# The transfers of a chunked recurrence through DRAM, moved from ACT's queue to GpSimd's with another scratch layout, in a two-layer trunk on one core

## The chip, the cores and the metric

The kernel runs on one core of a Trainium2 chip. What counts is the device time of one execution in microseconds. The engines are PE (matrix products), DVE (vector work), ACT (scalar work and casts), GpSimd, which the profile calls POOL, and SP, which here issues DMAs only. A DMA is issued by an instruction in the queue of one engine and carried out by 16 DMA engines that all queues share.

## What is computed

The input x has 256 rows of 2048 values in f32. Layer 0 adds a mixer of two kinds of heads, layer 1 a dilated attention, and each layer ends with an MLP of inner width 8192:

```python
for l in range(DEPTH):                    # DEPTH = 2
    if l % 2 == 0:
        x = x + diff_delta_mixer(rms_norm(x, ab_norm[i]), ...)
    else:
        x = x + dilated_mixer(rms_norm(x, c_norm[i]), ...)
    x = x + squared_relu_mlp(rms_norm(x, mlp_norm[l]), mlp_w1[l], mlp_w2[l])
```

The part that the change touches is the gated delta rule of the 8 "b" heads of layer 0, in chunks (cut):

```python
m = jnp.einsum('bhncd,bhnjd->bhncj', kb, k) * decay_strict
sol = lax.linalg.triangular_solve(eye + m, rhs, left_side=True, lower=True, unit_diagonal=True)
u, w = sol[..., :dv], sol[..., dv:]
def step(state, xs): ...                  # the state goes from chunk to chunk
```

## The kernel before

All dense products run through `dense` (L191): the weights are loaded by `wload` (L171) on SP's queue, cast on ACT to a high part (L204, tiles ending in h) and on DVE to a low part (L205, shown as L107 since the helper `tt` stands there, tiles ending in l), and each chunk of 128 rows takes six matmuls of 128x512 on PE (L210 to L212). High and low parts have six buffers each. After each chunk `drip` (L182) runs one step of the side work, which is held as generators in three streams. A scheduler then puts the instructions of each engine in an order of its own; each engine works through its own order strictly.

The recurrence is the generator `gdn` (L594), called four times (s = 0 to 3, tiles g0.. to g3..), each for two heads and two blocks of 128 rows, so four matrices of 128x128. A call goes as follows. `dd` holds the decays: a row of cumulative gates, written to DRAM once as scg (L530), is read back to all partitions (L623). `pk` is the product of the keys with themselves, and DVE makes `m` from it (L648). `m` is written to the scratch scm in DRAM (L651) and its 16x16 blocks on the diagonal, 8 to a matrix and 32 in all, are read into `mb`, one block to a partition (four DMAs, L654). DVE inverts the 32 blocks (`xc`, L673 to L695; a copy at L695 makes the transposed half). The inverses and their transposes are written into the block diagonals of the scratch scx, which was filled with zeros in `gates` (L534 to L536), by eight DMAs (L698), and the whole of scx is read back as `xy` (L704). From there three levels of PE products (`lp`, `ly`, `lx`, L720 on) build the whole inverse; the first is `lp16`, named g0lp and so on in the profile. Before the change all these DMAs are issued by ACT, whose queue also holds the casts of the weights. scm and scx are tiles of 128 partitions in which the four matrices (and in scx both halves) stand side by side in a row, so that a block diagonal is one pattern only per matrix.

The names beside it: z0, av0, av1, a1, wo00 are dense products of the mixer, c0 to c3 the convolutions (side work, with small memsets on GpSimd), d0 to d3 the other kind of heads (large memsets d0kb to d3kb on GpSimd), xq the input tiles, ca the constants, grow a row of gains, b0 the first dense product.

Of the kernel before, what the change touches and what calls it, by code (L numbers as in the profile page):

```python
# [11 lines left out]
F32 = mybir.dt.float32  # L12
# [7 lines left out]
P = 128  # L20
# [7 lines left out]
BLK = 16  # L28
# [59 lines left out]
def trunk(  # L88
# [4 lines left out]
    nc = tc.nc  # L93
    V, S, G, E = nc.vector, nc.scalar, nc.gpsimd, nc.tensor
# [5 lines left out]
    dp = ctx.enter_context(tc.tile_pool(name="dp", bufs=1, space=bass.MemoryType.DRAM))  # L100
# [5 lines left out]
    def tt(o, a, b, op):  # L106
        V.tensor_tensor(out=o, in0=a, in1=b, op=op)  # L107

    def vcopy(o, a):
        V.tensor_copy(out=o, in_=a)  # L110

    def stt(o, a, s, b, op0, op1):
        V.scalar_tensor_tensor(out=o, in0=a, scalar=s, in1=b, op0=op0, op1=op1)

    def ts(o, a, s1, s2, op0, op1=None):
        if op1 is None:
            V.tensor_scalar(out=o, in0=a, scalar1=s1, scalar2=None, op0=op0)
        else:
            V.tensor_scalar(out=o, in0=a, scalar1=s1, scalar2=s2, op0=op0, op1=op1)

    def act(o, a, f, scale=1.0, bias=0.0, accum=None):
        if accum is None:
            S.activation(out=o, in_=a, func=f, scale=scale, bias=bias)  # L123
        else:
            S.activation(out=o, in_=a, func=f, scale=scale, bias=bias, accum_out=accum)
# [4 lines left out]
    def ps_t(name):  # L130
        return pst.tile([P, 512], F32, tag="t", name=name)

    def ps_m(name):
        return psm.tile([P, 512], F32, tag="m", name=name)
# [36 lines left out]
    def wload(wsrc, k0, nm):  # L171
        raw = wp.tile([P, 2, 512], F32, tag="wr", name=f"{nm}r{k0}")
        off = 0
        for s in wsrc:
            m = s.shape[1]
            nc.sync.dma_start(raw[:, :, off:off + m], s[k0 * P:(k0 + 2) * P, :].rearrange("(c p) n -> p c n", p=P))
            off += m
        return raw
# [47 lines left out]
    ca = cp.tile([P, NMAIN], F32, name="ca")  # L226

    def cst(name):
        lo, hi = COLS[name]
        return ca[:, lo:hi]  # L230
# [3 lines left out]
    def transpose(o, i, k=P):  # L234
        E.transpose(o, i, ident[:k, :k])
# [12 lines left out]
    def x_tile(n, nm):  # L248
        return cp.tile([P, NH, 512], F32, tag=f"x{n}", name=f"{nm}{n}")
# [93 lines left out]
    xv = x[0].rearrange("(h p) d -> p h d", p=P)  # L343
# [3 lines left out]
    def b_cols(s):  # L347
        return [win[:, 3072 + s * 256:3328 + s * 256], win[:, 4096 + s * 256:4352 + s * 256]]

    grow0 = sp.tile([16, P], F32, tag="junk", name="grow0")  # L350
# [8 lines left out]
    xq = [x_tile(n, "xq") for n in range(4)]  # L359
    pre = []  # L360
    for n in range(4):
        if n == 0:
            nc.sync.dma_start(xq[0][:, :, :256], xv[:, :, :256])
            nc.sync.dma_start(ca[:, :P], consts[:, :P])
            nc.sync.dma_start(grow0, ab_norm[0].rearrange("(c p) -> c p", p=P))
            nc.sync.dma_start(xq[0][:, :, 256:], xv[:, :, 256:512])
        else:
            nc.sync.dma_start(xq[n], xv[:, :, n * 512:(n + 1) * 512])
        if n < 3:
            pre.append(wload(b_cols(0), 2 * n, "b0"))  # L370
    with ExitStack() as mix:
        wq[0] = mix.enter_context(tc.tile_pool(name="wq0", bufs=1))
        op = mix.enter_context(tc.tile_pool(name="op", bufs=1))
# [87 lines left out]
        gout = gt[:, 65:66]  # L461
        ready = set()
        oa, ob = [None] * 4, [None] * 4
        scm = [dp.tile([P, 512], F32, name=f"scm{i}") for i in range(2)]
        scg = dp.tile([16, P], F32, name="scg")
        scx = [dp.tile([P, 1024], F32, name=f"scx{i}") for i in range(2)]


        sz = [None] * NH
# [16 lines left out]
        def flat(a):  # L486
            return a.rearrange("p h n -> p (h n)")

        def gates(a, b):
            ts(beta, b, 0.5, 0.5, ALU.mult, ALU.add)  # L490
            ts(nbeta, beta, -1.0, None, ALU.mult)
            tt(a, a, dtb.unsqueeze(1).broadcast_to([P, NH, 8]), ALU.add)

            ab = mp.tile([P, NH, 8], F32, name="gab")
            y = mp.tile([P, NH, 8], F32, name="gy")
            w = mp.tile([P, NH, 8], F32, name="gw")
            q = mp.tile([P, NH, 8], F32, name="gq")
            stt(ab, a, -1.0, a, ALU.mult, ALU.min)
            act(y, ab, AF.Exp)
            ts(w, y, 2.0, None, ALU.add)  # L500
            V.reciprocal(out=w, in_=w)
            tt(w, y, w, ALU.mult)
            tt(y, w, w, ALU.mult)
            ts(q, y, 1.0 / 17.0, 1.0 / 15.0, ALU.mult, ALU.add)
            for d in (13, 11, 9, 7, 5, 3, 1):
                tt(q, q, y, ALU.mult)
                ts(q, q, 1.0 / d, None, ALU.add)
            yield
            tt(q, q, w, ALU.mult)
            ts(a, a, 0.0, None, ALU.max)  # L510
            stt(a, q, 2.0, a, ALU.mult, ALU.add)
            tt(gg, a, nega.unsqueeze(1).broadcast_to([P, NH, 8]), ALU.mult)
            yield
            yield
            pc = ps_m("pgc")
            E.matmul(pc[:, 0:16], lhsT=cst("tri"), rhs=flat(gg), start=True, stop=True)
            E.matmul(pc[:, 16:32], lhsT=cst("ones"), rhs=flat(gg), start=True, stop=True)
            vcopy(flat(gc), pc[:, 0:16])
            act(flat(egc), pc[:, 0:16], AF.Exp)
            e = sp.tile([P, 16], F32, tag="rs_z", name="ge")  # L520
            tt(e, pc[:, 16:32], flat(gc), ALU.subtract)
            act(flat(egl), e, AF.Exp)
            ngc = sp.tile([P, 16], F32, tag="ngc", name="ngc")
            ts(ngc, flat(gc), -1.0, None, ALU.mult)
            yield
            pc = ps_t("pgt")
            transpose(pc[:16, :P], ngc)
            row = sp.tile([P, 512], F32, tag="junk", name="grow_t")[:16, :P]
            vcopy(row, pc[:16, :P])
            nc.scalar.dma_start(scg, row)  # L530
            ready.add("gates")
            yield
            zero = mp.tile([P, 1024], F32, tag="xy", name="zero")
            G.memset(zero, 0.0)  # L534
            for z in scx:
                nc.sync.dma_start(z, zero)  # L536
            yield
            ready.add("zero")

# [54 lines left out]
        def gdn(qks, s, vb, nm):  # L594

            def mt(tag, n=4, share=None):
                return mp.tile([P, n, P], F32, tag="g_" + (share or tag), name=nm + tag)
# [19 lines left out]
            for i in range(4):  # L617
# [2 lines left out]
            ts(sq, rs[:, 4:8], 128.0 ** -0.5, None, ALU.mult)  # L620

            dd = mt("dd")
            nc.scalar.dma_start(  # L623
                dd.rearrange("p (h e) c -> p h e c", h=NH),
                bass.AP(scg.tensor, scg.offset + 2 * s * P, [[0, P], [8 * P, NH], [P, 2], [1, P]]))
            for i, (h, e) in enumerate(tiles):
# [6 lines left out]
            t = ps_t(nm + "kt")  # L633
# [8 lines left out]
            m, am = mt("m"), mt("am")  # L642
# [5 lines left out]
                stt(m[:, i, :], pk[:, i * P:(i + 1) * P], nbeta[:, h, hd:hd + 1], dd[:, i, :], ALU.mult, ALU.mult)  # L648

            scr, sxy = scm[s % 2], scx[s % 2]  # L650
            nc.scalar.dma_start(scr, m.rearrange("p i c -> p (i c)"))  # L651
            mb = mp.tile([32, BLK, BLK], F32, tag="g_mb", name=nm + "mb")
            for i in range(4):
                nc.scalar.dma_start(  # L654
                    mb[i * 8:(i + 1) * 8],
                    bass.AP(scr.tensor, scr.offset + i * P, [[BLK * 512 + BLK, 8], [512, BLK], [1, BLK]]))
            yield
            mT, aT = mt("mT"), mt("aT")
            t = ps_t(nm + "tt1")
# [5 lines left out]
            xc = mp.tile([32, 2, BLK, BLK], F32, tag="g_P", name=nm + "xc")  # L665
# [9 lines left out]
            for j in range(3):  # L675
                n, w = 3 - j, j + 1
# [16 lines left out]
                if b == 4:  # L693
                    yield
            vcopy(xc[:, 1].rearrange("p r c -> p c r"), x0)  # L695
            for i in range(4):
                for q in range(2):
                    nc.scalar.dma_start(  # L698
                        bass.AP(sxy.tensor, sxy.offset + q * 512 + i * P,
                                [[BLK * 1024 + BLK, 8], [1024, BLK], [1, BLK]]),  # L700
                        xc[i * 8:(i + 1) * 8, q])

            xy = mp.tile([P, 2, 4, P], F32, tag="xy", name=nm + "xy")
            nc.scalar.dma_start(xy.rearrange("p q i c -> p (q i c)"), sxy)  # L704
            X, Y = xy[:, 0], xy[:, 1]
            yield
            pa = ps_m(nm + "pa")
# [5 lines left out]
            t = ps_t(nm + "tt2")  # L713
# [5 lines left out]
            for li, b in enumerate(LEVELS):  # L719
                t = ps_m(f"{nm}lp{b}")  # L720
# [5 lines left out]
                t = ps_m(f"{nm}ly{b}")  # L726
# [4 lines left out]
                t = ps_t(f"{nm}lx{b}")  # L731
# [4 lines left out]
            t = ps_m(nm + "lpz")  # L736
# [5 lines left out]
            t = ps_m(nm + "lyz")  # L742
# [7 lines left out]
            t = ps_m(nm + "pu")  # L750
# [3 lines left out]
            t = ps_m(nm + "pw")  # L754
# [5 lines left out]
            t = ps_m(nm + "ps")  # L760
# [7 lines left out]
            t = ps_m(nm + "pv")  # L768
# [9 lines left out]
            t = ps_m(nm + "po")  # L778
# [406 lines left out]
```

## Time and profile before

| | |
|---|---|
| median of three runs | 2303.09 us (2300.97 to 2303.63) |
| the profiled execution | 2305.11 us, its span 2303.4 us |
| busy: PE / DVE / ACT / GpSimd | 2285.2 / 1666.8 / 1192.3 / 5.6 us |
| mean granted TensorE clock | 0.998 |
| DMA traffic | 426.54 MB, of it 4.60 MB on ACT's queue |

The span is the time between the first and the last record of the profiled execution; that execution took 1.7 us more than its span. Busy times are sums over the whole program. A view of stretches gives the busy time of each engine in a window, so that a window's length less PE's busy time is PE's idle time there; PEclk is the TensorE clock granted in it, as a share of full speed. The timeline gives single instructions, and for an instruction that issues a DMA the time of the issue, not of the transfer. The four recurrences lie between 75 and 450 us, the rest is other dense work and the two MLPs.

### The profile page before, as it was taken

Reading aid. Unit: us, or ns where it says so; the run is one execution under the profiler, and the core shown is the slowest. Engines: PE = TensorE matmul, PEld = TensorE weight load, DVE = VectorE, ACT = ScalarE, POOL = GpSimd, SP = SyncE. Lnnn points to the kernel's source line nnn. Section 1 sums busy time; section 2 is a strip of 40 time slices with the busy share of each in tenths; the row PEclk is TensorE's granted clock in tenths of the full one; section 3 lists DMA queues with packets and bytes.
Section 4 is the critical chain, followed back from the end, with each engine's and each line's share of the span. In section 5 each row is a group of like instructions: output and inputs, shape, how many; then the busy total and the mean of one; then the engine's idle time right before and its main releaser. Section 6 shows DMA issues by size and latency. Waiting matters only on the chain.

```text
span 2303.4 us, 29959 instructions
## 1 busy us (share of the span) xinstructions
PE 2285.2 (99%) x10544; PEld 1891.9 (82%) x10544; DVE 1666.8 (72%) x3027; ACT 1192.3 (52%) x1865; POOL 5.6 (0%) x15
## 2 busy tenths in 40 slices
PE   9999999999999999999999999999999999999999
PEld 8887878788888888888888888888888888888887
DVE  6767787777856856856888888986775775775774
ACT  7656756655534534534545555555543543443553
POOL 0000000000000000000000000000000000000000
PEclk9999999999999999999999999999999999999999
DMA  8655554466666666666666555555666666666665
GB/s 257 186 173 152 148 166 143 129 192 176 192 199 191 190 196 194 189 200 192 189 195 200 174 182 170 176 185 166 193 193 195 192 194 193 190 197 195 188 208 164
DMA packets 264762, 426.54 MB, mean 185 GB/s; under 512 B 22514, under 2 KB 94372, under 8 KB 264612
## 3 DMA queue, kind: packets, MB, share of 16 engines
q1 hardware_dynamic: 255812, 420.04, 60.0%
q10 hardware_dynamic: 8800, 4.60, 0.7%
q8 instruction: 82, 1.34, 0.3%
q14 instruction: 68, 0.56, 0.1%
HBM read 420.11 MB, written 4.46 MB: 184 GB/s over the span
## 4 chain that ended last, share of the span: by engine, by line
PE 92%; DVE 4%; DMA 2%; ACT 1%; issue 0%; ACTq 0%; SPq 0%; DVEq 0%
PE m_0p L211 3%; PE m_0p L212 3%; PE n_0p L212 3%; PE m_1p L210 3%; PE m_3p L210 3%; PE m_2p L210 3%; PE n_1p L212 3%; PE m_3p L212 3%; PE n_2p L211 3%; PE m_1p L212 3%; PE n_1p L211 3%; PE m_2p L212 3%; PE n_0p L210 3%; PE n_2p L210 3%; PE n_2p L212 3%; PE n_1p L210 3%
## 5 line engine op out<-in xcount | busy, mean ns | idle before, releaser
L107 DVE TENSOR_TENSOR n_2l<-n_2r,n_2h 128x1024 fp32r<-128x1024 f32 x64 | 78.4, 1226 | 76.8 <-ACT n_2h L204 76.7
L107 DVE TENSOR_TENSOR n_3l<-n_3r,n_3h 128x1024 fp32r<-128x1024 f32 x64 | 78.4, 1225 | 76.7 <-ACT n_3h L204 76.6
L107 DVE TENSOR_TENSOR m_0l<-m_0r,m_0h 128x1024 fp32r<-128x1024 f32 x64 | 78.1, 1225 | 73.4 <-ACT m_0h L204 73.0
L107 DVE TENSOR_TENSOR n_1l<-n_1r,n_1h 128x1024 fp32r<-128x1024 f32 x64 | 78.4, 1224 | 67.7 <-ACT n_1h L204 67.2
L204 ACT CAST n_2h<-n_2r 128x1024 fp32r<-128x1024 f32 x64 | 67.4, 1053 | 100.3 <-PE n_2p L212 61.6
L204 ACT CAST n_3h<-n_3r 128x1024 fp32r<-128x1024 f32 x64 | 67.3, 1052 | 100.2 <-PE n_3p L212 60.0
L204 ACT CAST m_0h<-m_0r 128x1024 fp32r<-128x1024 f32 x64 | 67.0, 1053 | 97.3 <-PE m_0p L212 59.9
L204 ACT CAST n_1h<-n_1r 128x1024 fp32r<-128x1024 f32 x64 | 67.4, 1053 | 92.8 <-PE n_1p L212 60.0
L107 DVE TENSOR_TENSOR m_1l<-m_1r,m_1h 128x1024 fp32r<-128x1024 f32 x64 | 78.4, 1225 | 36.9 <-ACT m_1h L204 35.9
L204 ACT CAST m_1h<-m_1r 128x1024 fp32r<-128x1024 f32 x64 | 67.4, 1053 | 66.6 <-PE m_1p L212 38.3
L204 ACT CAST m_3h<-m_3r 128x1024 fp32r<-128x1024 f32 x64 | 67.4, 1053 | 57.4 <-PE m_3p L212 39.9
L204 ACT CAST n_0h<-n_0r 128x1024 fp32r<-128x1024 f32 x64 | 67.4, 1053 | 57.3 <-PE n_0p L212 39.9
L204 ACT CAST m_2h<-m_2r 128x1024 fp32r<-128x1024 f32 x64 | 67.4, 1053 | 57.3 <-PE m_2p L212 39.9
L107 DVE TENSOR_TENSOR m_3l<-m_3r,m_3h 128x1024 fp32r<-128x1024 f32 x64 | 78.4, 1225 | 25.7 <-ACT m_3h L204 24.3
L107 DVE TENSOR_TENSOR n_0l<-n_0r,n_0h 128x1024 fp32r<-128x1024 f32 x64 | 78.4, 1225 | 25.7 <-ACT n_0h L204 24.0
L107 DVE TENSOR_TENSOR m_2l<-m_2r,m_2h 128x1024 fp32r<-128x1024 f32 x64 | 78.4, 1225 | 25.7 <-ACT m_2h L204 23.8
L293 DVE STREAM_TRANSPOSE m_0hT<-m_0r 32x256 f32<-32x256 f32 x128 | 55.8, 436 | 5.8 <-ACT m_0r L123 3.7
L293 DVE STREAM_TRANSPOSE m_2hT<-m_2r 32x256 f32<-32x256 f32 x128 | 55.8, 436 | 5.7 <-ACT m_2r L123 3.6
L293 DVE STREAM_TRANSPOSE m_3hT<-m_3r 32x256 f32<-32x256 f32 x128 | 55.8, 436 | 5.7 <-ACT m_3r L123 3.6
L293 DVE STREAM_TRANSPOSE m_1hT<-m_1r 32x256 f32<-32x256 f32 x128 | 55.8, 436 | 5.7 <-ACT m_1r L123 3.6
L210 PE MATMUL n_0p<-n_0h,m_3hh 128*128 128x512 f32 x64 | 24.9, 389 | 0.0
L210 PE MATMUL n_3p<-n_3h,m_1hh 128*128 128x512 f32 x64 | 24.9, 389 | 0.0
(2555 smaller groups left out, 7401.0 us busy)
## 6 DMA issues: line engine op xcount, KB each, us to landing
m_0r<-in_mlp_w_dram SPq DMA_DIRECT2D x64, 512.0 KB
m_1r<-in_mlp_w_dram SPq DMA_DIRECT2D x64, 512.0 KB
m_2r<-in_mlp_w_dram SPq DMA_DIRECT2D x64, 512.0 KB
m_3r<-in_mlp_w_dram SPq DMA_DIRECT2D x64, 512.0 KB
n_0r<-in_mlp_w_dram SPq DMA_DIRECT2D x64, 512.0 KB
n_1r<-in_mlp_w_dram SPq DMA_DIRECT2D x64, 512.0 KB
n_2r<-in_mlp_w_dram SPq DMA_DIRECT2D x64, 512.0 KB
n_3r<-in_mlp_w_dram SPq DMA_DIRECT2D x64, 512.0 KB
```

What stands on the lines that cost most here:

```text
L107: V.tensor_tensor(out=o, in0=a, in1=b, op=op)
L204: cast[0] = S.copy(whs, w)
L210: E.matmul(o, lhsT=sh, rhs=wh, start=kc == first, stop=False)
L211: E.matmul(o, lhsT=sh, rhs=wl, start=False, stop=False)
L212: E.matmul(o, lhsT=sl, rhs=wh, start=False, stop=kc == last)
L293: V.transpose(out=dv[:, :, :, q], in_=sv[:, :, :, j, :])
```

## The change

At the head, the loads of ca and grow go to ACT's queue, and the second half of the first input tile is issued after the first weights. In the mixer the scratch tiles become rows of images: scm has four and scx eight images of 128x128 with a pad of 128 behind each, so that the step from one block to the next on the diagonal also leads from the last block of one image to the first of the next. With that, all 32 blocks are one pattern (`DIAG`), the four reads of mb one DMA and the eight writes of scx two. The writes and reads of whole images now have runs of 512 B. All DMAs of the recurrence (scg, dd, scm, mb, scx, xy) are issued by GpSimd (`G`). For each call of `gdn` these are 15 DMAs before and 6 after.

```diff
-            nc.sync.dma_start(ca[:, :P], consts[:, :P])
-            nc.sync.dma_start(grow0, ab_norm[0].rearrange("(c p) -> c p", p=P))
-            nc.sync.dma_start(xq[0][:, :, 256:], xv[:, :, 256:512])
+            nc.scalar.dma_start(ca[:, :P], consts[:, :P])
+            nc.scalar.dma_start(grow0, ab_norm[0].rearrange("(c p) -> c p", p=P))
...
+        if n == 0:
+            nc.sync.dma_start(xq[0][:, :, 256:], xv[:, :, 256:512])
...
-        scm = [dp.tile([P, 512], F32, name=f"scm{i}") for i in range(2)]
+        IMG, DIAG = P * P + P, [[BLK * (P + 1), 32], [P, BLK], [1, BLK]]
+        scm = [dp.tile([4, IMG], F32, name=f"scm{i}") for i in range(2)]
-        scx = [dp.tile([P, 1024], F32, name=f"scx{i}") for i in range(2)]
+        scx = [dp.tile([8, IMG], F32, name=f"scx{i}") for i in range(2)]
+        def images(t):
+            return t[:, :P * P].rearrange("i (p c) -> p i c", c=P)
...
-            nc.scalar.dma_start(scg, row)
+            G.dma_start(scg, row)
...
-                nc.sync.dma_start(z, zero)
+                nc.sync.dma_start(images(z), zero.rearrange("p (i c) -> p i c", c=P))
...
-            nc.scalar.dma_start(
+            G.dma_start(
                 dd.rearrange("p (h e) c -> p h e c", h=NH),
...
-            nc.scalar.dma_start(scr, m.rearrange("p i c -> p (i c)"))
+            G.dma_start(images(scr), m)
-            for i in range(4):
-                nc.scalar.dma_start(
-                    mb[i * 8:(i + 1) * 8],
-                    bass.AP(scr.tensor, scr.offset + i * P, [[BLK * 512 + BLK, 8], [512, BLK], [1, BLK]]))
+            G.dma_start(mb, bass.AP(scr.tensor, scr.offset, DIAG))
...
-            for i in range(4):
-                for q in range(2):
-                    nc.scalar.dma_start(
-                        bass.AP(sxy.tensor, sxy.offset + q * 512 + i * P,
-                                [[BLK * 1024 + BLK, 8], [1024, BLK], [1, BLK]]),
-                        xc[i * 8:(i + 1) * 8, q])
+            for q in range(2):
+                G.dma_start(bass.AP(sxy.tensor, sxy.offset + q * 4 * IMG, DIAG), xc[:, q])
-            nc.scalar.dma_start(xy.rearrange("p q i c -> p (q i c)"), sxy)
+            G.dma_start(xy.rearrange("p q i c -> p (q i) c"), images(sxy))
```

The order of the instructions changes with it. On PE, around the first matmul of `lp16` in the third call (g2lp; av1p is the output of the dense product av1, av1h and av1l its weights), before:

```order
L210 MATMUL av1p_3628<-av1h_3840,xa3h 128x512
L211 MATMUL av1p_3628<-av1l_3841,xa3h 128x512
L212 MATMUL av1p_3628<-av1h_3840,xa3l 128x512
L210 MATMUL av1p_3627<-av1h_3857,xa3h 128x512 [waits Activation_49]
L722 MATMUL g2lp_3739<-g2xy,g2mT 128x128 [waits DMAHW6_49]
L722 MATMUL g2lp_3739<-g2xy,g2mT 128x128 x3
L211 MATMUL av1p_3627<-av1l_3858,xa3h 128x512 [waits DVE_49]
```

and after, on the same engine at the same matmul:

```order
L210 MATMUL av1p_3601<-av1h_3719,xa1h 128x512
L211 MATMUL av1p_3601<-av1l_3720,xa1h 128x512
L212 MATMUL av1p_3601<-av1h_3719,xa1l 128x512
L721 MATMUL g2lp_3712<-g2xy,g2mT 128x128 [waits DMASW3_49]
L721 MATMUL g2lp_3712<-g2xy,g2mT 128x128 x3
L210 MATMUL av1p_3600<-av1h_3735,xa2h 128x512 [waits Activation_49]
L211 MATMUL av1p_3600<-av1l_3736,xa2h 128x512 [waits DVE_49]
```

Before, the product stood among the last quarter of av1 (input block xa3); after, it stands between its second and third quarter (xa1 and xa2). From `pk` of the same call to this place there are 145 dense matmuls before and 114 after; in g0 118 and 108, in g1 108 and 108, in g3 95 and 73.

On ACT, around the scatters of the third call, before (8x16x16 is one of the eight writes of scx, CAST are high parts of av1):

```order
L204 CAST av1h_3778<-av1r_3760 128x512 [waits DVE_49,PE_49]
L698 DMA scx_228<-g2xc 8x16x16 [waits DMAHW4_49,DVE_49]
L698 DMA scx_228<-g2xc 8x16x16 [waits DMAHW5_49,DVE_49]
L698 DMA scx_228<-g2xc 8x16x16 x2
L698 DMA scx_228<-g2xc 8x16x16 [waits DMAHW2_49]
L698 DMA scx_228<-g2xc 8x16x16 [waits DMAHW3_49]
L698 DMA scx_228<-g2xc 8x16x16 [waits DMAHW4_49]
L698 DMA scx_228<-g2xc 8x16x16 [waits DMAHW5_49]
L204 CAST av1h_3793<-av1r_3791 128x512 [waits DMAHW1_49,PE_49]
```

and on GpSimd after, the rows of the third call:

```order
L657 DMA scm_225<-g2m 128x4x128 [waits DVE_49]
L877 MEMSET d1kb 128x1024 [waits DVE_49,Pool_49]
L659 DMA g2mb<-scm_225 32x16x16 [waits DMASW6_49,DMASW1_49]
L629 DMA g3dd<-scg 128x2x256 [waits DMASW2_49,DVE_49]
L700 DMA scx_228<-g2xc 32x16x16 [waits DVE_49] x2
L703 DMA g2xy<-scx_228 128x8x128 [waits DMASW2_49,DMASW5_49,DMASW1_49,PE_49]
```

The scatters stand no longer between two casts; on GpSimd they stand behind a memset and the load of the next call's decays. In the first call `g1dd` stands between the scatters and g0xy in the same way, in the second `g2dd` ahead of the scatters. ACT's order holds no DMA behind the head any more.

## Rows read from the trace of the kernel before

**Rows 1.** The page: busy us of the engines, share of the span, instructions.

```profile
PE 2285.2 (99%) x10544; PEld 1891.9 (82%) x10544; DVE 1666.8 (72%) x3027; ACT 1192.3 (52%) x1865; POOL 5.6 (0%) x15
```

**Rows 2.** Stretches of 25 us: length, PE, PEld, DVE, ACT, POOL busy, PEclk, DMA share, GB/s.

```profile
0.00:25.00 25.00, 22.56 (x114) 18.56 (x115) 15.98 (x32) 17.59 (x40) 1.20 (x6) 1.00 0.89 290
300.00:325.00 25.00, 21.89 (x99) 17.01 (x97) 20.54 (x62) 11.77 (x21) 0.00 (x0) 1.00 0.62 181
325.00:350.00 25.00, 24.46 (x125) 19.82 (x126) 17.57 (x44) 15.95 (x43) 0.95 (x1) 0.93 0.52 165
400.00:425.00 25.00, 21.27 (x86) 15.78 (x85) 17.75 (x56) 11.70 (x29) 0.95 (x1) 0.86 0.30 95
```

**Rows 3.** The same view from `pk` to `lp16` in g0, g1, g2, g3.

```profile
100.34:133.16 32.82, 31.69 (x160) 25.90 (x158) 28.39 (x64) 18.43 (x34) 0.76 (x2) 1.00 0.58 172
189.78:225.98 36.20, 34.47 (x174) 27.39 (x173) 29.03 (x89) 20.11 (x50) 0.11 (x1) 1.00 0.57 164
288.90:330.90 42.00, 38.35 (x170) 30.51 (x169) 37.13 (x95) 18.55 (x31) 0.95 (x1) 0.96 0.64 189
386.70:424.80 38.10, 34.31 (x153) 26.00 (x152) 28.12 (x91) 18.48 (x46) 0.95 (x1) 0.91 0.39 123
```

**Rows 4.** Timeline of ACT in g2, its DMA issues: start us, us, what.

```profile
296.00 0.35 ACTq L651 DMA_DIRECT2D scm<-g2m  x1
299.09 1.45 ACTq L654 DMA_DIRECT2D g2mb<-scm  x4
317.29 3.96 ACTq L698 DMA_DIRECT2D scx<-g2xc  x8
323.71 0.35 ACTq L704 DMA_DIRECT2D g2xy<-scx  x1
```

**Rows 5.** Instructions of tile g2xc: durations in ns, first and last start in us.

```profile
L113 DVE SCALAR_TENSOR_TENSOR g2xc<-g2mb,ca x1: 415/415/415, 306.2 to 306.2; 32x256 f32<-32x256 f32 x1
L110 DVE COPY g2xc<-g2xc x1: 368/368/368, 317.8 to 317.8; 32x256 f32<-32x256 f32 x1
```

**Rows 6.** The chain of three stretches (head, g0, g2): start us, us, what.

```profile
3.68 6.25 DMA xq<-in_x_dram
108.41 0.23 PE z0p L210
128.54 4.57 DMA g0xy<-scx
312.19 1.05 DVE g2tm L107
313.23 0.60 DVE av1l L107
```

**Rows 7.** Waits of ACT, then of PE: us in total, times, longest.

```profile
ACT av1h L204 <- DVE d1uw L107: 8.2, 1, 8.2
PE av1p L211 <- DVE av1l L107: 3.2, 2, 2.8
```

**Rows 8.** ACT's DMA queue, 121.7:128.6, 136.2:141, 128.5:133.3 us: packets, MB, share.

```profile
q10 hardware_dynamic: 1088, 0.07, 10.6%
q10 hardware_dynamic: 272, 0.26, 18.1%
q10 hardware_dynamic: 144, 0.52, 28.4%
```

**Rows 9.** GpSimd's instructions by shape: busy us, mean ns, idle before.

```profile
L878 POOL MEMSET d1kb<- 128x1024 f32 x1 | 1.0, 955 | 38.6 <-DVE qk L113 38.6
L534 POOL MEMSET zero<- 128x1024 f32 x1 | 1.0, 951 | 0.0
L553 POOL MEMSET c0x<- 128x16 f32 x1 | 0.1, 111 | 0.3 <-POOLq L1171 0.3
```

**Rows 10.** Timeline of the SP queue in the head: start us, us, what.

```profile
1.22 0.46 SPq L364 DMA_DIRECT2D ca<-in_consts_dram  x1
3.68 0.47 SPq L368 DMA_DIRECT2D xq<-in_x_dram  x1
```

## What the change will do to the time: the prediction

> **What bounds the kernel now.** I read the page first, then the busy time of 25-us stretches, then the stretches around the four recurrences, and only then the waits in them. TensorE (PE) is busy 2285.2 of 2303.4 us [rows 1]: what makes PE wait counts, nothing else does. The stretches say where PE is not busy: 2.4 us in the first 25 us, then 3.1, 0.5 and 3.7 us and a lowered clock around the third and fourth recurrence [rows 2]; these stretches hold over half of PE's 18.2 us of idle time. The change touches just these two places, the head and the four calls of `gdn` (g0 to g3), and the rest of the span I take as a constant.
>
> In each call I take the stretch from the start of `pk`, the first matmul of the recurrence, to the first matmul of `lp16`, which needs what comes back from DRAM: 32.8, 36.2, 42.0 and 38.1 us, with PE busy 31.7, 34.5, 38.4 and 34.3 of them [rows 3]. The reader is to see that two things run side by side there. One is PE's other work, the dense matmuls put ahead of `lp16`. The other is a chain: `pk`, `m`, write of scm, reads of mb, the triangular inverse on DVE (xc), writes of scx, read of xy. The later of the two sets the time.
>
> **The chain, in g2.** scm is issued at 296.00, 7.1 us after the start of the stretch; the first mb read at 299.09 (A, 3.1 us); xc begins on DVE at 306.17 (B, 7.1); its last copy starts at 317.8 and takes 0.37 (C, 12.0 from the start); xy is issued at 323.71 (D, 5.5) [rows 3 to 5]. A read of xy took 4.57 in g0 (E) [rows 6]; I use 4.6. What the transfers cost is S = A+B+D+E = 20.3 us. The same sum for g0, g1 and g3 (three calls, same lines) is 17.9, 19.3 and 18.7. The time from the start of the stretch to the scm issue is 3.2, 5.6, 7.1 and 5.2. In g2 xy had landed by 328.3 and `lp16` came at 330.9: there the chain was hidden behind dense work.
>
> **What the change does to S, link by link.** A: 512 packets of 512 B in place of 128 of 2 KB. The scatters' packets of 64 B took 10.7 ns each (10.6% of 16 engines for 6.9 us over 1088) and the 272 packets of dd, nearly all of 1 KB, 51 ns (18.1% of 16 engines for 4.8 us) [rows 8]; xy's 144 took 21.8 us in all, 151 ns each. Between the first two, 512 packets on 16 engines are 0.3 to 1.6 us; 128 at half of xy's price are 0.6 now. I take +0.5. B: four issues become one; they took 1.45 for four [rows 4], so -1.1. The runs stay 64 B. D: eight issues become two, 3.96 us in all with a wait at the first [rows 4]; six fewer at about 0.33 are -1.9. E: 1024 packets of 512 B in place of 128 of 4 KB; by the same rows 0.7 to 3.3 us against 1.4 now, so -0.7 to +1.9; I take +0.8. So far -1.7.
>
> Then the engine that issues. No row shows a DMA issued by GpSimd; its own instructions take 0.11 us for a small memset and 0.955 for a large one [rows 9], an issue on ACT 0.35 [rows 4]. Four issues lie one behind the other in the chain (scm, mb, the second scatter, xy). At 0.11 they give back 1.0 us, at 0.955 they cost 2.4. I take the upper end, since each DMA has 512 or 1024 pieces, which is nearer to the memset that writes much. S then goes up by 0.7 a call. The bounds: S-4.0 (A and E unchanged, GpSimd at 0.11), and S+4.9 from the rival on DVE below.
>
> Descriptor cost as the Trainium skill has it ("DMA: Bandwidth & Descriptors", Latency and other measured facts): about 1 us to the first byte from GpSimd, about 0.6 from ACT. By it four links would cost 1.6 rather than 2.4 and the total would come out about 3 us lower; no run here shows it.
>
> **What it does to C.** Inside g2's xc the changed order has five casts av1l where before had seven; at 0.60 each [rows 6] that is -1.2, and the other pieces that move in and out make about -0.5 (an estimate from their rows, 0.26 to 0.66 each). C becomes about 10.2 in g2 and, counted in the same way, 10.3, 10.0 and 10.0 in g0, g1 and g3.
>
> **What it does to PE's side.** This is the part that decides. With the transfers taken for shorter, the order puts `lp16` earlier among the dense matmuls: in g2 114 of them stand between `pk` and `lp16` where 145 stood, in g0 108 for 118, in g3 73 for 95 (and three small ones more), in g1 108 as before. At 0.23 a matmul [rows 6] that is 7.1, 2.3, 4.4 and 0 us less work ahead of `lp16`, and the same work behind it. PE's side becomes 29.4, 34.5, 31.2 and 29.9 us for g0 to g3. Everything on PE behind `lp16` queues when it waits, dense work too, and DVE's P16 with the casts behind it.
>
> **ACT.** Its queue was held at the scatters. The longest of these waits, 8.2 us in g2, is put down to d1uw, but the cast that ends it stands behind the eight scatters in the queue [rows 7]; PE then starved 3.2 us for av1l [rows 7]. That wait goes. What is late next is `lp16`, so nothing of the 3.2 is gained in g2. GpSimd's queue: `g1dd` stands ahead of `g0xy`, `g2dd` ahead of g1's scatters, `g3dd` ahead of g2's. In before g3dd's issue was long over when the scatters came, so I price these at nothing; if one waits, all behind it waits.
>
> **The head.** xq1's issue, from which the first wait that counts hangs, is the seventh on its queue at 3.68; ca and grow leave that queue, about 0.5 each with the gap behind [rows 10], so it comes about 1.0 us earlier. Its landing (6.25 us later [rows 6]) shares full DMA engines, so I take -0.8, bounds 0 and -1.0.
>
> **The sum.** Chain with S+0.7, that is (start to scm) + C + S + 0.7: g0 32.1, g1 35.6, g2 38.3, g3 34.6. Each is above PE's side, so PE waits 2.7, 1.1, 7.1 and 4.7 us. Adding the work moved behind (2.3, 0, 7.1, 4.4) gives 34.4, 35.6, 45.4 and 39.0 against 32.8, 36.2, 42.0 and 38.1: +1.6, -0.6, +3.4 and +0.9, together +5.3. A wait of over 3 us was followed by a lower granted clock (325 to 350 us at 0.93, 1.7 us lost [rows 2]); two such waits, +3.4. With the head -0.8 that is +7.9. The profiled execution was 2305.11 with span 2303.4, the median of three 2303.09; I add the sum to the median: 2311.0.
>
> **The rivals.** (1) The GpSimd issue is quick. With S-4.0 the chains are 27.4, 31.0, 33.6 and 29.9, PE's side sets g0, g1 and g3, and the stretches become 31.7, 34.5, 40.7 and 34.3: -7.9, with the head -8.7, no long wait left: 2294.4. For it speaks that GpSimd is idle and ACT's stops disappear; against it the longer lists of packets. It decides at about S-2.6, where the sum falls below -0.2%. (2) A wash: S-1.5, with mb and scx landing as now and the issue at about 0.35. Chains 29.9, 33.4, 36.1 and 32.4, stretches 32.2, 34.5, 43.2 and 36.8, -2.4; one long wait +1.7, the head -0.8: 2301.6. (3) GpSimd is held while DVE works. Each of the four links falls behind one DVE instruction of up to 1.05 us [rows 6], +4.2 a call, S+4.9. Chains 36.3, 39.8, 42.5, 38.8; stretches +22; long waits in all four, +6.8; with the head +28: 2331. Against it: the large memset on GpSimd took 0.955 in g2's stretch (d1kb), where DVE is busy 37.1 of 42.0 us, and 0.951 at the start of the kernel (zero), where it has little to do [rows 3, 9].
>
> The Trainium skill has this last case as a rule ("SBUF — State Buffer", SBUF: two separate sides): while DVE runs an operation on both ports, GpSimd is locked out of the port they share and cannot write descriptors, and it advises issuing from ACT or SP. The memset's row does not bear it out for these DVE operations, which is why the chance is small; no transfer here shows it.
>
> **How the numbers follow.** Forecast 0.42 (S from -1 to +3, 2304 to 2322), quick GpSimd 0.26, wash 0.20, DVE lock 0.12. Below 2294 I leave about 5%, above 2330 about 10%; the range is 2294 to 2330. For the forecast alone it would be 2304 to 2322. A measurement tells about 0.2% (4.6 us). Faster by more: all of (1) and a little of (2), 0.30. Slower by more: (3) and most of the forecast, 0.45. The rest, 0.25, is the same.
>
> **What would show it.** The page after: PE's idle grows before `lp16` in g2 and g3 and ends on the xy transfer, not on av1l; ACT no longer waits for scx. The time from scm's issue to xc's start and from xc's copy to xy's landing gives S directly: 21.0 in g2 if I am right, 16.3 if quick, 25 if locked. The lengths of GpSimd's DMA rows price the issue. xa1t should start near 9.3 us. Wrong would be: S well below 20 in g2, `lp16` finding xy landed, or a dd load on GpSimd's queue that waits and holds the scatters behind it.

## The result, and the profile after

| | before | changed kernel |
|---|---|---|
| median | 2303.09 us (2300.97 to 2303.88, 5 runs) | 2312.21 us (2311.34 to 2314.96, 5 runs) |
| ratio | 1 | 1.0041, 95% interval 1.0028 to 1.0054 |
| profiled execution, its span | 2305.11, 2303.4 us | 2311.34, 2309.6 us |

The changed kernel is 0.41% slower, 9.1 us by the medians and 6.2 us by the two profiled executions. The forecast was 2311.0. Two executions further down lie far off and are left out, one of gp_lp_later (3854 us) and one of sp_issues (6363 us), on which its profile fell, so that no time is read from the trace of sp_issues.

The page of the changed kernel, its first section, against [rows 1]; PE's busy time is the same, its idle time is 24.5 us where it was 18.2, and that makes up the 6.2 us between the two spans:

```profile
PE 2285.1 (99%) x10544; PEld 1892.8 (82%) x10544; DVE 1666.2 (72%) x3027; ACT 1196.0 (52%) x1865; POOL 23.9 (1%) x40
```

Stretches of 25 us of the changed kernel, columns as in [rows 2]:

```profile
0.00:25.00 25.00, 23.02 (x111) 19.65 (x112) 15.33 (x31) 16.95 (x37) 1.20 (x6) 1.00 0.88 285
100.00:125.00 25.00, 20.23 (x106) 16.35 (x105) 21.43 (x55) 12.42 (x22) 2.85 (x5) 0.97 0.51 151
125.00:150.00 25.00, 25.00 (x116) 20.98 (x117) 17.34 (x32) 12.32 (x20) 2.58 (x3) 0.90 0.62 191
...
325.00:350.00 25.00, 19.75 (x99) 16.13 (x98) 16.15 (x47) 10.84 (x27) 0.90 (x1) 0.93 0.49 147
```

There is a loss at 100 to 150 us that [rows 2] had no place for: PE stands 4.8 us, and then the granted clock falls, in finer stretches to 0.50 from 124 to 130 us. The stretches from `pk` to `lp16` of the four calls, answering [rows 3]:

```profile
100.70:137.70 37.00, 32.23 (x150) 26.19 (x149) 31.24 (x73) 19.38 (x33) 5.43 (x8) 0.91 0.58 172
196.50:233.40 36.90, 34.97 (x175) 27.39 (x174) 31.55 (x101) 24.78 (x63) 4.47 (x7) 1.00 0.63 188
296.10:331.50 35.40, 29.36 (x141) 23.86 (x139) 31.27 (x83) 16.98 (x28) 5.51 (x7) 1.00 0.69 207
396.00:426.70 30.70, 26.80 (x137) 20.49 (x135) 27.89 (x89) 19.48 (x50) 4.59 (x6) 1.00 0.44 133
```

With the work moved behind `lp16` (2.3, 0, 7.1, 4.4 us) these are 39.3, 36.9, 42.5 and 35.1 against 32.8, 36.2, 42.0 and 38.1: +6.5, +0.7, +0.5 and -3.0. The clock has a part in this: over the stretch of g0 it fell from 1.00 to 0.91, over that of g3 it rose from 0.91 to 1.00, each worth some 3 us. The first starts of dense products say the same. `z2p`, behind the head, is 0.7 us later than before; `a0p`, behind g0, 6.9; `b3p`, behind g1, 7.3; `a2p`, behind g2, 9.2; `wo10p`, behind g3, 5.9, and there it stays to the end. So g0 costs 6.2, g1 0.4, g2 1.9, g3 and the mixer's end give 3.3 back. What PE waits for, from the waits of the changed kernel (us in total, times, longest), against the last line of [rows 7]:

```profile
PE g2lp L721 <- DMA g2xy<-scx: 5.2, 1, 5.2
PE g0tt L235 <- DVE g0am L107: 3.5, 1, 3.5
PE d2at L235 <- DVE d2aa L113: 2.3, 1, 2.3
...
PE g3lp L721 <- DMA g3xy<-scx: 1.2, 1, 1.2
```

The wait for av1l is gone and g2lp waits for xy, as forecast. The largest loss, g0tt, is another one.

GpSimd's timeline in g2 (start us, us, what, in brackets the idle time before), against [rows 4], and below it two lines of the instructions of g2xc (ns, first and last start), against [rows 5]:

```profile
303.35 0.77 POOL L657 DMA_DIRECT2D scm<-g2m  x1 [37.02 <-DVE g2m L113]
304.91 0.96 POOL L877 MEMSET d1kb<- 128x1024 f32 x1 [0.79 <-DVE qk L113]
306.55 0.67 POOL L659 DMA_DIRECT2D g2mb<-scm  x1 [0.68 <-DMA scm<-g2m]
313.57 0.71 POOL L629 DMA_DIRECT2D g3dd<-scg  x1 [6.36 <-DVE g2xc L107]
321.43 1.54 POOL L700 DMA_DIRECT2D scx<-g2xc  x2 [7.15 <-DVE g2xc L128]
326.53 0.90 POOL L703 DMA_DIRECT2D g2xy<-scx  x1 [3.56 <-PE av1p L212]
```

```profile
L113 DVE SCALAR_TENSOR_TENSOR g2xc<-g2mb,ca x1: 412/412/412, 311.4 to 311.4; 32x256 f32<-32x256 f32 x1
L110 DVE COPY g2xc<-g2xc x1: 366/366/366, 321.7 to 321.7; 32x256 f32<-32x256 f32 x1
```

A is 3.2, B 4.9, C 10.7, D 4.4, and xy lands 4.9 us after its issue: S is 17.4 where it was 20.3. In the same way g0, g1 and g3 have 16.4, 19.2 and 15.5 where they had 17.9, 19.3 and 18.7. **S did not rise by 0.7 a call, it fell by 1.9 on average**, and the kernel is slower nevertheless. (The 4.6 in each sum of before is xy's time in g0. The last packets on ACT's queue put xy's landing at some 3.3, 3.3 and 6.1 us in g1, g2 and g3; with that g2 had 19.0, and the average fell by 1.7.) The memset in this timeline delays the read of mb by nothing: it ends at 305.87, and the read still waits 0.68 for scm.

### The profile page after: what moved, and what is told of

The parts are those of the page before. It is cut to its first block, busy times and chain, and to the rows that moved or that the text cites. A ratio compares the mean times of both kernels' runs of the same rounds, so it can differ in the third digit from the quotient of the medians.

```text
span 2309.6 us, 29934 instructions
## 1 busy us (share of the span) xinstructions
PE 2285.1 (99%) x10544; PEld 1892.8 (82%) x10544; DVE 1666.2 (72%) x3027; ACT 1196.0 (52%) x1865; POOL 23.9 (1%) x40
## 4 chain that ended last, share of the span: by engine, by line
PE 85%; issue 2%; DVE 2%; DMA 1%; ACT 0%; POOL 0%; POOLq 0%; ACTq 0%; DVEq 0%
PE m_0p L211 3%; PE n_2p L212 3%; PE n_1p L212 3%; PE n_0p L210 3%; PE m_3p L210 3%; PE m_2p L211 3%; PE m_2p L210 3%; PE m_1p L211 3%; PE m_1p L210 3%; PE m_3p L211 3%; PE n_1p L210 3%; PE n_2p L211 3%; PE n_0p L212 3%; PE m_0p L212 3%; PE n_0p L211 3%; PE n_2p L210 3%
## 5 line engine op out<-in xcount | busy, mean ns | idle before, releaser
L107 DVE TENSOR_TENSOR m_1l<-m_1r,m_1h 128x1024 fp32r<-128x1024 f32 x64 | 78.4, 1225 | 36.9 <-ACT m_1h L204 35.9
L210 PE MATMUL n_0p<-n_0h,m_0hh 128*128 128x512 f32 x64 | 24.9, 389 | 0.0
L211 PE MATMUL n_0p<-n_0l,m_0hh 128*128 128x512 f32 x64 | 24.9, 389 | 0.0
```

Of the source, the lines that this page charges most:

```text
L210: E.matmul(o, lhsT=sh, rhs=wh, start=kc == first, stop=False)
L211: E.matmul(o, lhsT=sh, rhs=wl, start=False, stop=False)
```

## Experiments

Each kernel was timed beside runs of the kernel before on the same chip; their medians are 2303.83 (head, act_issues, tt2_later), 2303.39 (gp_dd, gp_in, gp_out and old_layout_gp) and 2303.93 (the last four). Each kernel has one trace; those of act_issues and gp_dd are of executions 2.3 and 2.7 us below their medians, so a difference of 1 or 2 us between single traces need not be one of the kernels. Short names: "the issuer" is the engine that issues scm, mb, scx and xy.

**1. The head: old_head and new_head.** old_head is the changed kernel with the head of before; new_head is the kernel before with

```diff
-            nc.sync.dma_start(ca[:, :P], consts[:, :P])
-            nc.sync.dma_start(grow0, ab_norm[0].rearrange("(c p) -> c p", p=P))
-            nc.sync.dma_start(xq[0][:, :, 256:], xv[:, :, 256:512])
+            nc.scalar.dma_start(ca[:, :P], consts[:, :P])
+            nc.scalar.dma_start(grow0, ab_norm[0].rearrange("(c p) -> c p", p=P))
...
+        if n == 0:
+            nc.sync.dma_start(xq[0][:, :, 256:], xv[:, :, 256:512])
```

> The changed kernel with the loads of ca, grow and the second half of xq0 put back as before; the mixer's order is that of the changed kernel, row for row. The trace of the changed kernel shows the first dense matmul 1.1 us later than before and PE 0.7 us behind from 34 us on. Theory (the head lost 0.7, everything else comes from the mixer): some 0.7 us under the changed kernel, 2311.5, xa1t back at 10.1 us and PE at z2p at 34.0. The forecast's step (the head gains 0.8): 2313.

> The kernel before with the new head alone; the order of the mixer is that of before. Theory: +0.7 us, 2303.8, z2p at 34.7 us. The forecast's step: -0.8, 2302.3, z2p at 33.2. The time itself can hardly tell these apart, the start of z2p in the trace can.

Measured: old_head 2311.45 (2310.99 to 2313.45), new_head 2303.14, ratio 0.9998 (0.9989 to 1.0007). `z2p` started at 33.9 us in old_head's trace, as before; at 32.9 in new_head's, where the changed kernel with the same head had 34.7. Both expectations for new_head's trace fall: one code gave 1.1 us less and 0.7 us more. The chain there runs through the landing of input tiles, which differs from execution to execution: in the ten traces with the old head `z2p` starts between 33.3 and 34.2 us. The head is worth nothing that these runs can tell.

**2. The issuer: act_issues.** The new layout and the order that comes with it, the old head, and ACT as the issuer:

```diff
-            G.dma_start(images(scr), m)
+            nc.scalar.dma_start(images(scr), m)
-            G.dma_start(mb, bass.AP(scr.tensor, scr.offset, DIAG))
+            nc.scalar.dma_start(mb, bass.AP(scr.tensor, scr.offset, DIAG))
```

and so for scg, dd, scx and xy.

> The new scratch layout and the old head, but all six transfers of a call issued by ACT; PE's order from pk to lp16 is that of the changed kernel in g0, g1 and g2 (tt2 and lp16 at the same places) and within a few matmuls of it in g3. Theory A, the order costs: PE waits for am at g0tt2 by 2 us or more, then runs at the lower clock, and waits at g2lp for xy by 3 us or more, though GpSimd issues nothing: 2307 to 2312. Theory B, the issue by GpSimd costs: these waits fall under 1 us and the time goes back to 2303 or below.

Measured: 2299.47 (2297.18 to 2302.51, 11 runs), ratio 0.9981 (0.9972 to 0.9989), 12.0 us under old_head, which differs in the issuer and in what the scheduler made of it. PE's order from `pk` to `lp16` is the same in g0 and g2, has tt2 and `lp16` at the same places in g1, and in g3 has 81 dense matmuls ahead of `lp16` for 73; DVE's and ACT's orders moved too (in g0 am stands ahead of xc's copy on DVE, in old_head behind it and one more cast). Theory A, PE's order alone, falls: in nearly the same order the kernel is faster than before. Theory B has the time right, but not the waits, which are halved and not gone. Waits of PE in act_issues:

```profile
PE g2lp L720 <- DMA g2xy<-scx: 2.9, 1, 2.9
PE g0tt L235 <- DVE g0am L107: 1.8, 1, 1.8
PE d2at L235 <- DVE d2aa L113: 1.6, 1, 1.6
```

ACT's timeline in g2 shows what the layout brings by itself and what GpSimd takes back:

```profile
295.07 0.38 ACTq L656 DMA_DIRECT2D scm<-g2m  x1
298.12 0.33 ACTq L658 DMA_DIRECT2D g2mb<-scm  x1
311.43 1.21 ACTq L699 DMA_DIRECT2D scx<-g2xc  x2
314.12 0.38 ACTq L702 DMA_DIRECT2D g2xy<-scx  x1
```

xc began at 301.6 and its copy, 0.37 long, at 311.9; xy landed 5.8 us after its issue. So S is 3.0+3.5+1.8+5.8 = 14.1 us here, 20.3 before and, in old_head, 18.2. Over the four calls S is 19.1 on average before (18.9 with xy's landings by the packets), 14.3 with the new layout on ACT, 17.9 in old_head. **The layout takes 4.5 to 4.8 us off a call, and the issue by GpSimd puts 3.5 back.** Of the 3.5, up to 1.9 are the five issue rows of a call, each longer on GpSimd by 0.3 to 0.5; the rest is in later landings, above all of the last scatter: 1.7 to 3.1 us after its issue by ACT, 2.1 to 5.6 by GpSimd.

**3. Which transfers: gp_dd, gp_in, gp_out.** Three kernels that give GpSimd one group each in act_issues: scg and dd; scm and mb; scx and xy. The edits are those of the change, group by group. PE's order from `pk` to `lp16` stays that of act_issues within a few matmuls; DVE's does not in all of them (gp_in has that of the changed kernel in g0).

> As act_issues (new layout, old head, ACT issues), but the write of scg and the four loads of dd issued by GpSimd; PE's order from pk to lp16 is that of act_issues. In the trace of the changed kernel DVE stood 2.2 us for g0dd (0.2 with ACT), so that vb, m and am came 2 us later and PE waited 3.5 us at g0tt2 and then ran at the lower clock. Theory 1 (dd on GpSimd starts that chain of delays): +4 to +7 us over act_issues, 2304 to 2306, g0tt2 waits over 3 us. Theory 2 (only the links from scm to xy cost): same as act_issues, 2299 to 2300.

> As act_issues, but the write of scm and the read of mb issued by GpSimd; PE's order from pk to lp16 is that of act_issues but for one step in g3. From the issue of scm to the start of xc the changed kernel took 7.4 us on average, act_issues 6.8. Both theories: 0 to +3 us over act_issues, 2299.5 to 2302.5.

> As act_issues, but the scatters into scx and the read of xy issued by GpSimd; PE's order from pk to lp16 is that of act_issues within one matmul. From xc's copy to xy's landing old_head took 9.9 us on average, act_issues 7.6. Theory 1: g2lp waits 2 us more for xy, g3lp up to 1: +2 to +4, 2301.5 to 2303.5. Theory 2: nearly the whole difference, +8 to +12, 2307 to 2311.

| | median | over act_issues | ratio to before |
|---|---|---|---|
| gp_dd | 2299.85 | +0.4 | 0.9985 (0.9976 to 0.9994) |
| gp_in | 2304.59 | +5.1 | 1.0005 (0.9996 to 1.0014) |
| gp_out | 2305.22 | +5.8 | 1.0007 (0.9998 to 1.0016) |

The three sum to 11.3 of the 12.0 us, so no large interaction is seen, though each difference is uncertain by some 2 us. gp_dd is where Theory 1 falls: g0tt waited 2.6 us there and `a0p` came 2.4 us later than in act_issues, but the mixer's end was where act_issues has it (`wo10p` at 467.8 and 467.7): a delay of g0 that is regained in g2 and g3. In g2 it goes with the clock: from 300 to 325 us act_issues has 0.93 and gp_dd 1.00, and gp_dd is 1.6 us less behind after it (3.2 at `b3p`, 1.6 at `a2p`). What regains the rest wasn't tried. gp_in costs more than expected for 1.0 us more from scm to xc a call (7.7 for 6.8): in g0 xc begins 1.3 us later from `pk` and am, with DVE's other order, 1.7; g0tt waits 3.5 us, and the clock falls with it. Stretches of gp_in and, below, of gp_dd, columns as in [rows 2]:

```profile
100.00:125.00 25.00, 21.47 (x111) 17.87 (x110) 21.03 (x51) 11.42 (x22) 1.69 (x3) 0.94 0.51 144
```

```profile
100.00:125.00 25.00, 21.14 (x111) 17.10 (x110) 21.93 (x56) 12.32 (x23) 0.83 (x2) 1.00 0.55 150
```

PE is idle nearly as long in both, but only in gp_in does the granted clock drop. gp_out lengthens the way from xc's copy to xy's landing by 2.8 us a call (10.4 for 7.6), and g2lp and g3lp wait for it (4.5 and 2.2 us), with the clock at 0.91 to 0.95 in the stretches around them. It also falls in g0, where the wait at g0tt is 1.8 us as in act_issues, whose clock stays up; gp_out and, below, act_issues:

```profile
100.00:125.00 25.00, 23.15 (x115) 19.19 (x114) 22.40 (x54) 12.67 (x24) 1.62 (x3) 0.93 0.58 168
```

```profile
100.00:125.00 25.00, 23.18 (x121) 19.29 (x120) 22.57 (x55) 12.54 (x24) 0.11 (x1) 1.00 0.57 158
```

Of the 8.0 us between the spans of these two traces, 4.9 are PE busy for longer with the same matmuls (2284.8 for 2279.9) and 3.1 are idle: most of gp_out's price in its trace is time at the lower clock.

**4. GpSimd with the old layout: old_layout_gp.** The kernel before, with `nc.scalar` replaced by `G` in the 15 transfers of a call and in scg.

> The kernel before with its scratch layout and its 15 transfers a call, all issued by GpSimd (scg too); the order on PE is a third one (lp16 1 us later than before in g0, 1 us earlier in g2, 2.5 us later in g3). GpSimd's issues took 0.65 us at the least in the changed kernel whatever the size, ACT's 0.34. If the price is one of each issue, six more issues a call of 0.65 lie in the chain from xc to xy: D over 7 us where before has 5.3 to 5.9, and the time is 2310 to 2320. If the price is one of the number of pieces, small DMAs of 128 pieces are as quick as on ACT and the time is 2302 to 2308.

Measured: 2310.41 (2308.62 to 2318.26, 8 runs), ratio 1.0035 (1.0025 to 1.0045). D was 7.7, 8.3, 7.4 and 8.3 us. GpSimd's timeline in g2:

```profile
301.92 0.57 POOL L651 DMA_DIRECT2D scm<-g2m  x1 [37.01 <-DVE g2m L113]
...
305.40 2.43 POOL L654 DMA_DIRECT2D g2mb<-scm  x4 [0.96 <-DMA scm<-g2m]
...
322.26 5.01 POOL L698 DMA_DIRECT2D scx<-g2xc  x8 [11.60 <-DVE g2xc L128]
330.31 0.58 POOL L704 DMA_DIRECT2D g2xy<-scx  x1 [3.04 <-DMA scx<-g2xc]
```

The price is mostly one of each issue: 0.57 to 0.65 us for one of 128 pieces, 0.65 to 0.77 for 512 and 0.90 for 1024, with a few longer ones. On ACT nearly all issues took 0.27 to 0.38 in either layout. So fewer DMAs do help GpSimd: S is 22.6 a call with 15 and 17.9 with 6. The time is the same within the intervals; this order puts `lp16` later.

**5. The order: tt2_later, gp_lp_later, act_tt2_head, act_later.** `gdn` gives way to the dense work by `yield`; more of them ahead of tt2 (the transposes of am) or of `lp16` put these later on PE. From the changed kernel with the old head, tt2_later:

```diff
             tt(am, quads(pa), dd, ALU.mult)
-            for _ in range(1):
+            for _ in range(3):
                 yield
...
-            for _ in range(4):
+            for _ in range(2):
                 yield
             for li, b in enumerate(LEVELS):
```

gp_lp_later has 3 and 4 in these places; act_later is act_issues with 3 and 3, act_tt2_head is act_issues with 2 and 3 and the new head.

> The changed kernel with the old head and two more steps before the transposes of am (tt2), two fewer behind them: on PE tt2 moves back by 20 dense matmuls in g0 (some 4.6 us), lp16 stays where it is, DVE's order around xc is the same. All transfers as in the changed kernel, issued by GpSimd. Theory A (order): the 3.5 us wait at g0tt2 and the lowered clock behind it (3 us) go, 5 to 6 us under old_head: about 2306. Theory B (transfers): no change, as old_head.

> The changed kernel with the old head, GpSimd issues, and two more steps ahead of tt2 and two more ahead of lp16: on PE lp16 stands 5 us later in g0 and g1 and 8 us later in g2 than in the changed kernel (g3 comes out in another order). If what GpSimd costs is only that PE meets xy too early, the waits at g0tt2, g0lp and g2lp vanish and the time falls to 2303 or below. If the recurrence is late in any case, the time stays at 2307 to 2312, with the waits moved to later steps of the recurrence or to the end of the mixer.

> act_issues with two more steps ahead of tt2 and one fewer behind it, so lp16 stands about 2.8 us later in g0, g1 and g2. With ACT's issues the chain is short and g2lp waits 2.9 us for xy, which this takes away; g3 comes out in another order. Expected 2296 to 2300; if the later lp16 makes the mixer's end late, 2300 to 2304.

> act_issues with one more step ahead of tt2 and one fewer behind it (tt2 8 dense matmuls later in g0, lp16 in place) and the new head. In act_issues PE waits 1.8 us at g0tt2 and 2.9 at g2lp. Expected: the first wait goes, the clock does not drop behind it, the second stays; with the new head's -0.7 some 2 us under act_issues: 2297 to 2299. If both are noise: 2299 to 2300.

| issuer | kernel | median | ratio to before |
|---|---|---|---|
| GpSimd | old_head | 2311.45 | 1.0034 (1.0022 to 1.0047) |
| GpSimd | tt2_later | 2309.47 | 1.0028 (1.0017 to 1.0039) |
| GpSimd | gp_lp_later | 2303.45 | 0.9999 (0.9990 to 1.0008) |
| ACT | act_issues | 2299.47 | 0.9981 (0.9972 to 0.9989) |
| ACT | act_tt2_head | 2299.71 | 0.9985 (0.9976 to 0.9993) |
| ACT | act_later | 2299.91 | 0.9983 (0.9974 to 0.9991) |

tt2_later removes the wait at g0tt: `a0p` starts 4.5 us earlier than in old_head. But the gain is given back in part: g2lp waits 6.8 us for xy instead of 5.5, and 2.0 us are left by the medians, with intervals that overlap, not the 5 to 6 expected. With `lp16` later too, 8.0 us come off. Waits of PE in gp_lp_later, the first lines:

```profile
PE d3t L235 <- DVE d3qk L107: 1.8, 2, 1.3
PE d1t L235 <- DVE d1qk L107: 1.7, 2, 0.9
PE wo01p L211 <- DVE wo01l L107: 1.7, 1, 1.7
```

No product of the recurrence waits for a transfer any more. In act_issues a similar move is worth nothing: what PE waited at g2lp (2.9) it waits at d1t and g3lp instead (3.2 and 2.4 in act_later). So neither theory holds alone. GpSimd's chain is 3.5 us a call longer than ACT's, and the order of the changed kernel has no room for that; give it the room, and 8 of the 12 us come back.

**6. A third issuer: sp_issues.** As act_issues, with SP for scm, mb, scx and xy (`nc.sync` in their four places).

> New layout, old head, scm, mb, the scatters and xy issued by SP, scg and dd by ACT; PE's order as in act_issues within 5 dense matmuls. SP also issues the weight loads, which then stand behind the waits for m, scm, xc and scx. If a transfer is as quick from SP as from ACT and the weights are far enough ahead: 2298 to 2302, D about 2 to 3 us. If the weights run late: PE waits for casts of av1, a1 or wo00 and the time is above 2305.

Measured: 2294.89 us (2293.57 to 2296.14, 5 runs), ratio 0.9963 (0.9949 to 0.9976). It beats both kernels, and act_issues by 4.6 us. With no time from a trace, why it is better than ACT stays open: a freed ACT queue and another order (g0's tt2 1.0 us earlier, g2's `lp16` 1.1 us later by the count of matmuls) both fit. That the weights behind its waits would run late did not come true, by the time.

## Why the prediction was right, and where its steps were not

The time (2311.0 against 2312.2), the sign and the place of one loss were right. That the time came so near is luck: of the terms, S, the clock and g0 were wrong and offset each other. C, the work on DVE, held (10.6, 10.2, 10.6 and 9.7 against 10.3, 10.0, 10.2 and 10.0).

- **That PE would meet `lp16` too early in g2** held: it waits 5.2 us for xy (7.1 forecast), and the clock falls behind it. The stretch with the moved work is 42.5 against 42.0, and `a2p` shows 1.9 us lost in g2; 5.1 were forecast with the clock. The wait of g3lp is 1.2 and not 4.7, and g3 gives 3.0 us back instead of costing 0.9 and a clock dip. The waits are shorter because S is; what g3 gives back is the clock.
- **The clock: +3.4 was no net cost.** The forecast added two stretches at the lower clock and took none off, though before had two of its own ([rows 2]: 0.93 and 0.86; [rows 3]: 0.96 in g2, 0.91 in g3). The changed kernel has two as well, one in g0 and one behind g2's `lp16`, and none in g3; PE's busy time is 2285.1 us against 2285.2. The wait "of over 3 us" that the term was read from is two waits in [rows 7], the longer 2.8.
- **S: the term was mis-sized and its sign was wrong.** The links were to change by -1.7 without the issuer; act_issues measures -4.5 to -4.8. D was the worst: -1.9 was put down to six issues fewer, but D fell from 5.8 on average to 2.3 on ACT. In g2 the issues behind xc's copy went from 3.1 us to 0.4, and from the last issue's end to xy's issue it took 1.5 us where it had taken 2.5. B fell by 2.0 and not 1.1. Taking only the issues as saved, at 0.33 each, was the mistake.
- **The price of GpSimd's issue** was close: 0.95 a link was taken, 0.65 to 0.90 measured, but for all links together it is 3.5 us a call over ACT where 2.4 was forecast, since landings came later too. The choice of the upper end was right, but the reason (many pieces) explains only 0.3 of an issue; most is a fixed part.
- **g0 was missed.** The prediction counted where `lp16` moved, priced the dd loads at nothing and did not look at tt2, which moved up on PE by 2.8 us of matmuls in g0 (12 of them) while am came 1.9 us later: g0m is 1.9 us later from `pk`, since DVE stood 2.2 us for g0dd (0.6 before), whose write and read now both go through GpSimd. PE then stood 3.5 us and ran at 0.50 for some 5 us; the stretch is 6.5 us longer against 1.6 forecast. The dd loads that stand on GpSimd's queue beside the scatters held these by 0.6 us at the most (in g1).
- **ACT**: "what is late next is `lp16`" held for g2. The rival on DVE fell at its size: if GpSimd were held while DVE works, its issues would vary, but that of mb is 0.67 in all four calls, with DVE at work on TENSOR_TENSOR in each. One issue a call can be held: the first scatter took 0.86 us in g2, where xc's copy on DVE begins 0.2 us into it, and 0.65 to 0.67 in the other calls, where the copy begins with it or earlier. The rule that the Trainium skill has for this case ("SBUF — State Buffer", SBUF: two separate sides) is for operations of DVE on both ports, of which it names the f32 copy: the mb rows do not test it, and the 0.2 us at the copy agree with its sign. The first-byte difference of 0.4 us a DMA that the Trainium skill gives ("DMA: Bandwidth & Descriptors", Latency and other measured facts) is the size of the difference of the issue rows here, 0.3 to 0.5, but an issue row is not the time to a first byte, and no run here shows that time.
- **The head** was to give 0.8, with xa1t near 9.3 us; it started at 10.8 and, in new_head, at 8.9, and the runs with and without the head can't be told apart.

The sum was right because S came out 2.6 us a call lower than forecast and the clock cost nothing more, while g0 lost 4.6 us that were not in it and the head gave nothing. Of the rivals, the wash had S nearest (S-1.5 against -1.9) and the quick issue its sign (S-4.0). Put into the forecast's own sum, the measured S gives about 2300, a time below before; that the kernel is slower all the same is mostly g0.

What stays open: why the clock drops in g0 of gp_in and not of gp_dd, and in g0 of gp_out and not of act_issues, where PE is idle as long in the same stretch; and why SP is better than ACT. The orders that the scheduler made on DVE and ACT for each issuer were not held fixed, so the 12 us are those of the issuer together with them.

## What to carry to other kernels

When a change also moves instructions, list on the bound engine every instruction with a wait that has moved up, not only the one at the end of the chain, and set its new place against when its operand comes: here the second such place cost three times the first. A shorter chain of transfers is worth nothing if the order meets it earlier by more than it has become shorter, so layout, issuer and order are to be tried apart: the layout with its order was worth 4 us, its issue by GpSimd cost 12 (7 with the old layout), and 8 of the 12 came back when `lp16` and tt2 stood later. When a forecast adds time at a lower clock, take off what the kernel already loses to it. Moving issues to an idle engine frees the busy one, but look first at what one issue takes there.

## What the runs showed of the hardware that was not expected

- An issue by GpSimd depends little on what it carries: 0.57 us for 128 pieces of 2 KB, 0.67 for 512 of 64 B, 0.90 for 1024 of 512 B; on ACT 0.31 to 0.38 with the new layout.
- An f32 copy on DVE that begins 0.2 us into such an issue goes with a longer one: 0.86 to 0.87 us for the first scatter in all six such calls with the new layout (g2 of the changed kernel, old_head and tt2_later; g0, g1 and g2 of gp_out), 0.65 to 0.67 in the other calls of these and of gp_lp_later.
- GpSimd's queue is listed as another kind, and its packets are counted otherwise. The queues in g2 of the changed kernel (290 to 340 us) and of act_issues (290 to 325 us), which move the same bytes (packets, MB, share of 16 engines):

```profile
q0 software_dynamic: 400, 1.15, 9.1%
```

```profile
q10 hardware_dynamic: 3424, 1.15, 12.8%
```

- In g0 of the changed kernel PE came out of a wait of 3.5 us at the lower of the two clock levels (0.50 of full speed, 1.2 GHz) and stayed there for some 5 us. The length of this wait did not decide by itself: at the same place a wait of 2.6 us in gp_dd was followed by no drop, and one of 1.8 us was followed by a drop in gp_out (0.93 from 100 to 125 us) and by none in act_issues.
